# A hybrid decoder layer in f32: x, norm gains and conv weights come from the host in columns, and the norm of x and the k/v evacuation run as steps of the second product

## The chip, the cores and the metric

The kernel runs on one core of one Trainium2 chip. The metric is the time of one execution on the device, in microseconds (us); a kernel's figure is the median of its runs. Engines are named as in the profile: PE is TensorE (PEld its weight loads), DVE is VectorE, ACT is ScalarE, POOL is GpSimd, SP is SyncE. Loads and stores are put on a queue by an engine; in this kernel SP issues nearly all of them, POOL a few.

## The reference

One layer of a decoder, with all arrays in f32. x has 256 rows and 2048 columns. RMSNorm divides by the root of the mean square of a row and multiplies by a gain.

```python
h = rms_norm(x, norm_mix_pre)
c_q, c_kv, k_r, q_s, k_s, v_s, gates = split(h @ w_in)   # 512 | 256 | 64 | 2048 | 256 | 256 | 4096 columns
A = mla_attention(...)      # 16 heads from the latents c_q, c_kv; dense causal, rotary part
B = swa_attention(q_s, k_s, v_s, sinks, rel_bias)        # 32 heads on 4 k/v heads, window 128
y = (sigmoid(gA) * (A @ w_o_mla) + sigmoid(gB) * (B @ w_o_swa)) @ w_out
x = x + rms_norm(y, norm_mix_post)
a, b = split(rms_norm(x, norm_ffn_pre) @ w_up)           # 2 x 5632
c = conv_b + sum_j conv_w[j] * shift(a, 2 - j)           # causal, width 3
x = x + rms_norm((gelu(c) * b) @ w_down, norm_ffn_post)
```

## The kernel before

**Products.** Each f32 product is made of three products in the fp32r type: an operand is split into a rounded part (hi) and the rest (lo), and `mm3` (L142 to L145) adds hi times hi, lo times hi and hi times lo into one accumulator. In the profile's names the weights are `whi` and `wlo`, the activations `ah` and `al` (later bh, gh and so on), and L143, L144, L145 are the three products of a 128x128 activation tile with a 128x512 weight tile. The activations are the stationary operand, in columns: the features lie on the 128 partitions and the 256 rows of x are two tiles of 128 columns. So x has to be transposed before the first product.

**Weights.** `wchunk` (L101) issues the load of one piece of weights on SP's queue into a tile `raw<n>` (512 KB: two k-tiles of 128x512; n counts through the whole kernel), ACT copies it to `whi` (L118) and DVE subtracts to get `wlo` (L119). There are RAW = 3 raw tiles, so the load of raw n waits until the `wlo` of n-3 has been made, and RING = 5 tiles of whi and of wlo.

**The order.** `gemm` (L147) walks over the 16 k-tiles of one block of 512 weight columns: load, split, then 6 products per k-tile (two row tiles times three). After each load it calls `tick`, which runs what `at(n, ...)` put into the table `steps` for load n: the evacuations, small products and softmax pieces of other stages are placed between the loads in this way. On DVE, ACT and SP the written order holds inside the block `tc.manual_schedule`; elsewhere a scheduler orders the instructions by what they depend on, and `keep_in_program_order` holds single ones where they are written.

**The head,** which the change touches. Twelve small bf16 products (`warm_up`) run on PE while the first data come, then the gain of the first norm (`grow`, 16x128) is transposed into columns of `gmat` by `columns` (transpose on PE, L235, copy on DVE), then 15 more small products. The first product of the kernel, raw0 to raw8 (raw0 and raw1 hold one k-tile each, 256 KB), gives the k and v columns of the sliding-window attention (C_KS). x comes in rows as four tiles `xc` of 256x512 between the weight loads. For each k-tile, `x_cols` makes two transposes on PE (`xt`, L256), and `split_to` (L197) makes `ah` on ACT (times the gain, L203) and `al` on DVE. The norm's factor isn't needed for that: the row's 1/rms is multiplied into the results when they leave the accumulators. `x_square` (L246) takes the squares and their sums on ACT, one xc at a time, tile `junk`. Behind the product `x_norm` makes the factor r1 on DVE, transposes the other gains (`grow2`) and the conv weights (`cvr`, into `cvT`), and makes the relative-bias strip `strip` (product `pstrip`, L285, copy, store to DRAM, on POOL's queue; later read back shifted as `bias`, L377). Then k and v leave the accumulators as `kd` and `vs` (ACT L307 and L310, and a half of kd on DVE).

The second product, raw9 to raw16, is the first 512 of the 2048 q columns of the sliding-window attention. Steps in it: `swa_v(t)` (product `vr` with `flip`, which reverses the rows, L316, split into `vx`) at its loads 0 and 1, and `swa_k(g)` (products `kt`, L323, split into `kx`) at its loads 2 to 5. The third product starts with raw17.

The tiles of ah and al (`xth`, `xtl`) and those of later activations (`oth`, `otl`) are reserved one behind the other in `base`, with small unused tiles `line_a` (24 columns of 4 bytes) and `line_b` (8) between them, which set at which address the tiles behind them start.

Of the kernel before, what the change touches and what calls it, by code (L numbers as in the profile page):

```python
# [19 lines left out]
P = 128  # L20
# [21 lines left out]
def trunk_layer(ctx, tc, x, g_mix_pre, g_mix_post, g_ffn_pre, g_ffn_post, w_in, g_q, w_q, g_kv, w_kv,  # L42
                sinks, rel, wo_a, wo_b, w_out, w_up, conv_w, conv_b, w_down, rope_tab, strip_sel, out):
# [18 lines left out]

    ident = sb(base, [P, P], "ident")
# [23 lines left out]
    gmat = sb(base, [P, 40], "gmat")  # L87
# [121 lines left out]
    grow = sb(p0, [16, P], "grow")  # L209
    nc.sync.dma_start(grow, g_mix_pre.rearrange("(k p) -> k p", p=P))  # L210
    xc = []

    def load_x(c):
        t = sb(p0, [P, NT, 512], f"xc{c}")
        nc.sync.dma_start(t, x[:, c * 512:(c + 1) * 512].rearrange("(t p) n -> p t n", p=P))
        xc.append(t)

    load_x(0)
    grow2 = sb(p0, [24, P], "grow2")
    pool.dma_start(grow2[0:16, :], g_ffn_pre.rearrange("(k p) -> k p", p=P))  # L220
    pool.dma_start(grow2[16:20, :], g_q.rearrange("(k p) -> k p", p=P))
    pool.dma_start(grow2[20:22, :], g_kv.rearrange("(k p) -> k p", p=P))
    cvr = [sb(p0, [88, P], f"cvr{i}") for i in range(2)]
    cw3 = conv_w.rearrange("j (k p) -> j k p", p=P)
    pool.dma_start(cvr[0][0:44, :], cw3[0])
    pool.dma_start(cvr[0][44:88, :], cw3[1])
    pool.dma_start(cvr[1][0:44, :], cw3[2])
    pool.dma_start(cvr[1][44:88, :], conv_b.rearrange("(k p) -> k p", p=P))
    pool.dma_start(rtab, rope_tab.rearrange("(t p) a b -> p t a b", p=P))
    pool.dma_start(sink, sinks.partition_broadcast(P))  # L230
    cvT = sb(base, [P, 176], "cvT")

    def columns(dst, rows, n):
        pg = pss.tile([P, 512], F32, name=f"pg{rows.tensor.name}", tag="s")
        ins = pe.transpose(pg[:, 0:n], rows[0:n, :], ident[0:n, 0:n])  # L235
        tc.keep_in_program_order(ins)
        vec.tensor_copy(dst, pg[:, 0:n])

    sb(base, [P, 24], "line_a")
# [3 lines left out]

    def x_square(c):
        for t in range(NT):
            act.activation(junk, xc[c][:, t, :], AF.Square, accum_out=ssx[:, t, c:c + 1])  # L246

    def x_cols(k, ke):
        if k in (1, 6, 10):
            load_x(len(xc))  # L250
        if k and k % 4 == 0:
            x_square(k // 4 - 1)
        for k in range(k, ke):
            pt = (pst, pss)[k % 2].tile([P, 512], F32, name=f"xt{k}", tag="ts"[k % 2])
            for t in range(NT):
                ins = pe.transpose(pt[:, t * P:(t + 1) * P], xc[k // 4][:, t, (k % 4) * P:(k % 4 + 1) * P], ident)  # L256
                if k == 0:
                    tc.keep_in_program_order(ins)
            split_to(XH(k), XL(k), pt[:, 0:256], gmat[:, k:k + 1])
# [5 lines left out]
    junk = sb(p0, [P, 512], "junk", tag="junk", bufs=2)  # L265
# [7 lines left out]
    pool.dma_start(sel, strip_sel)  # L273

    def x_norm():
# [3 lines left out]
        columns(gmat[:, 16:38], grow2, 22)  # L279
        for i in range(2):  # L280
            columns(cvT[:, i * 88:(i + 1) * 88], cvr[i], 88)
        vec.tensor_scalar(r1s, r, 0.125, None, op0=ALU.mult)
        vec.tensor_scalar(rh, r, 0.5, None, op0=ALU.mult)
        pp = pss.tile([P, 512], F32, name="pstrip", tag="s")
        tc.keep_in_program_order(pe.matmul(pp[0:SH, 0:384], relx, sel, start=True, stop=True))  # L285
# [4 lines left out]
    with tc.manual_schedule(engines={mybir.EngineType.DVE, mybir.EngineType.Activation, mybir.EngineType.SP}):  # L290
        columns(gmat[:, 0:16], grow, 16)
        warm_up(WARM[1])
        acc, _ = gemm(XH, XL, w_in, 0, KT, C_KS, 512, pre=x_cols)
        x_square(3)
    r1 = x_norm()
    es0.close()


# [704 lines left out]
```

## Time and profile before

| | |
|---|---|
| median of 3 runs | 1501.5 us (1501.39 to 1504.84) |
| the profiled execution | 1502.09 us, span 1500.3 us |
| granted TensorE clock, mean | 0.998 |
| busy share of the span | PE 99%, PEld 83%, DVE 63%, ACT 53%, POOL 4% |
| moved by DMA | 285.46 MB, mean 190 GB/s |
| on the chain that ended last | PE 92%, DVE 3%, ACT 2%, DMA 2%, issue 1% |
| raw loads of 512 KB from w_in | 111 of this form, 4.2 us from issue to landing |

The span is what lies between the first and the last recorded instruction; the execution's time has 1.8 us around it. Busy times of matmuls overlap (a product is listed with 377 to 394 ns, though they follow each other faster), so a busy PE is not by itself a PE at its peak. The chain is followed back from the last instruction to what released each step. In tables of windows an engine's cell is its busy time with the count of instructions. In the timeline a line gives the start, the duration, the engine, the line of the kernel, the operation and tile, and in brackets what was waited for and how long.

### The profile page before, as it was taken

What the parts mean: (1) busy time and instruction counts of PE and PEld (TensorE: products, weight loads), DVE (VectorE), ACT (ScalarE), POOL (GpSimd) and SP (SyncE); (2) the same over time, 40 slices, a digit from 0 to 9 for tenths busy, and PEclk for the clock granted to TensorE, in tenths of its full rate; (3) what the DMA queues carried; (4) which work ended last, traced back from release to release, by engine and by line L of the source; (5) the groups of instructions that cost most, each with busy time, mean ns of one, the idle gap of its engine ahead of it and who ended that gap; (6) DMA issues with size and microseconds to landing.
All of it is one profiled execution on the core that took longest, in us unless ns stands there. A gap on an engine that the chain in (4) does not pass through costs nothing.

```text
span 1500.3 us, 20157 instructions
## 1 busy us (share of the span) xinstructions
PE 1483.9 (99%) x7347; PEld 1245.4 (83%) x7347; DVE 940.6 (63%) x1607; ACT 800.6 (53%) x1289; POOL 62.0 (4%) x105
## 2 busy tenths in 40 slices
PE   8999999999999999999999999999999999999997
PEld 6888887888899988888888888888888888888887
DVE  5688884444767764655666666666544466666755
ACT  6588874434555553444555555555444455545542
POOL 2123210000000001000000000000000000000000
PEclk9999999999999999999999999999999999999999
DMA  7776656776655559766656666665666666665563
GB/s 235 221 178 166 166 161 202 207 207 209 183 156 163 161 167 314 241 210 203 197 177 184 187 190 185 185 183 183 196 192 190 194 184 182 189 189 183 182 196 113
DMA packets 161748, 285.46 MB, mean 190 GB/s; under 512 B 18468, under 2 KB 33942, under 8 KB 161521
## 3 DMA queue, kind: packets, MB, share of 16 engines
q1 hardware_dynamic: 156464, 267.96, 59.2%
q0 software_dynamic: 5184, 16.22, 4.5%
q8 instruction: 58, 0.95, 0.3%
q14 instruction: 42, 0.34, 0.1%
HBM read 277.79 MB, written 6.34 MB: 189 GB/s over the span
## 4 chain that ended last, share of the span: by engine, by line
PE 92%; DVE 3%; ACT 2%; DMA 2%; issue 1%; SPq 0%; DVEq 0%; ACTq 0%
PE accg L145 27%; PE accg L144 27%; PE accg L143 27%; DMA raw<-in_w_in_dram 2%; PE fT L847 1%; DVE wlo L119 1%; PE mpo L681 1%; PE ms L647 1%; ACT p L407 1%; ACT whi L118 1%; PE qn L610 1%; PE qn L612 1%; PE qn L611 1%; PE ms L652 0%; PE ptm L365 0%
## 5 line engine op out<-in xcount | busy, mean ns | idle before, releaser
L119 DVE TENSOR_TENSOR wlo<-raw,whi 128x1024 fp32r<-128x1024 f32 (+2 forms) x501 | 609.1, 1217 | 482.9 <-ACT whi L118 482.1
L118 ACT CAST whi<-raw 128x1024 fp32r<-128x1024 f32 (+2 forms) x501 | 523.0, 1045 | 588.5 <-PE accg L145 500.2
L143 PE MATMUL accg<-whi,bh 128*128 128x512 f32 x960 | 377.9, 394 | 0.0
L145 PE MATMUL accg<-whi,bl 128*128 128x512 f32 x960 | 374.6, 390 | 0.0
L144 PE MATMUL accg<-wlo,bh 128*128 128x512 f32 x960 | 374.0, 390 | 0.0
L143 PE MATMUL accg<-whi,ah 128*128 128x512 f32 (+2 forms) x896 | 344.2, 385 | 0.7 <-ACT whi L118 0.7
L144 PE MATMUL accg<-wlo,ah 128*128 128x512 f32 (+2 forms) x896 | 341.4, 381 | 0.5 <-DVE wlo L119 0.5
L145 PE MATMUL accg<-whi,al 128*128 128x512 f32 (+2 forms) x896 | 340.9, 380 | 0.0
L145 PEld LDWEIGHTS accg<-whi,bl 128*128 128x128 f32 x960 | 180.2, 188 | 38.1
L144 PEld LDWEIGHTS accg<-wlo,bh 128*128 128x128 f32 x960 | 180.4, 188 | 36.4
L143 PEld LDWEIGHTS accg<-whi,bh 128*128 128x128 f32 x960 | 180.3, 188 | 36.0
L145 PEld LDWEIGHTS accg<-whi,al 128*128 128x128 f32 x896 | 168.5, 188 | 31.5
L144 PEld LDWEIGHTS accg<-wlo,ah 128*128 128x128 f32 x896 | 168.6, 188 | 30.8 <-DVE wlo L119 1.7
L143 PEld LDWEIGHTS accg<-whi,ah 128*128 128x128 f32 x896 | 168.5, 188 | 30.4 <-ACT whi L118 1.6
L143 PE MATMUL accg<-whi,gh 128*128 128x512 f32 (+1 forms) x104 | 39.3, 378 | 0.0
L144 PE MATMUL accg<-wlo,gh 128*128 128x512 f32 (+1 forms) x104 | 38.8, 373 | 0.0
L145 PE MATMUL accg<-whi,gl 128*128 128x512 f32 (+1 forms) x104 | 38.3, 373 | 0.0
L407 ACT ACTIVATE p<-p,nm 128x128 f32<-128x128 f32 x64 | 28.4, 445 | 5.9 <-DVE nm L398 5.9
L847 PEld LDWEIGHTS fT<-ident,f 128*128 128x128 f32 x176 | 21.8, 140 | 5.7
L847 PE MATMUL fT<-ident,f 128*128 128x128 f32 x176 | 26.3, 272 | 0.0
L851 ACT ACTIVATE cc<-fT,cvT 128x256 f32<-128x256 f32 x44 | 24.2, 550 | 0.0
L143 PEld LDWEIGHTS accg<-whi,gh 128*128 128x128 f32 x104 | 19.6, 188 | 4.1 <-ACT gh L200 0.9
(302 smaller groups left out, 1279.6 us busy)
## 6 DMA issues: line engine op xcount, KB each, us to landing
raw<-in_ffn_w_up_dram SPq DMA_DIRECT2D x176, 512.0 KB, 4.3
raw<-in_w_in_dram SPq DMA_DIRECT2D x111, 512.0 KB, 4.2
raw<-in_ffn_w_down_dram SPq DMA_DIRECT2D x88, 512.0 KB, 3.8
raw<-in_w_o_swa_dram SPq DMA_DIRECT2D x32, 512.0 KB, 4.2
raw<-in_w_o_mla_dram SPq DMA_DIRECT2D x32, 512.0 KB, 4.8
raw<-in_w_out_dram SPq DMA_DIRECT2D x32, 512.0 KB, 4.1
raw<-in_mla_w_q_up_dram SPq DMA_DIRECT2D x48, 128.0 KB, 2.9
bias<-strip POOLq DMA_DIRECT2D x16, 256.0 KB, 4.0
```

What stands on the lines that cost most here:

```text
L118: act.copy(hi[:, :n], raw[:, :n])
L119: vec.tensor_tensor(lo[:, :n], raw[:, :n], hi[:, :n].bitcast(F32), op=ALU.subtract)
L143: pe.matmul(o, ah, bh, start=start, stop=False)
L144: pe.matmul(o, ah, bl, start=False, stop=False)
L145: pe.matmul(o, al, bh, start=False, stop=stop)
L407: act.activation(pb[:, i, a:b], pb[:, i, a:b], AF.Exp, bias=st["nm"][:, i, t:t + 1], accum_out=st["sm"][:, i, t:t + 1])
L610: pe.matmul(o, wh, ch(k), start=k == 0, stop=False)
L611: pe.matmul(o, wh, cl(k), start=False, stop=False)
L612: pe.matmul(o, wl, ch(k), start=False, stop=k == nk - 1)
L647: pe.matmul(o, w, v_, start=n == 0, stop=False)
L847: pe.transpose(pt[:, q * 256 + t * P:q * 256 + (t + 1) * P], sa[t][q][:, i * P:(i + 1) * P], ident)
L851: act.activation(cc, a, AF.Identity, scale=w2, bias=cb_)
```

## The change

The host now hands over x a second time in columns (`x_cols`, 128 x 4096, all 2.10 MB), the four gains as one array of 128 x 38 (`gain_cols`) and the conv weights and bias as 128 x 176 (`conv_cols`). The tile `xr` takes x in columns, in pieces that fit the weight loads; gmat and the first two pieces are issued on ACT's queue, the others on SP's. ACT and DVE split from xr, where they split from the transposes' results before. x in rows (`xc`) is still loaded, for the squares alone, and later: beside raw5, raw6, raw7 and behind raw8. A copy of one column (`first`) stands first on ACT. All transposes of the head go, with the loads grow, grow2 and cvr and the copies behind them.

The squares of xc0 stand at the last piece of the first product; those of xc1, xc2 and xc3, the norm, and the evacuation of k and v become steps of the second product at its loads 0, 1, 2 and 3, `swa_v` moves to its loads 4 and 5, `swa_k` to 4 to 7. The written order now holds on DVE, ACT and SP from the kernel's start to the end of the first product. rtab (the rotary table) is loaded at step 4, cvT at step 20. The pads change: line_b from 8 to 32 columns, and a new line_w of 8 behind the tiles `oth` and `otl`. The tiles for activations start 32 bytes later than before, those for weights 160 bytes later.

```diff
@@ trunk_layer(...)
+    head = ExitStack()
+    head.enter_context(tc.manual_schedule(engines={mybir.EngineType.DVE, mybir.EngineType.Activation, mybir.EngineType.SP}))
...
-    grow = sb(p0, [16, P], "grow")
-    nc.sync.dma_start(grow, g_mix_pre.rearrange("(k p) -> k p", p=P))
+    xcut = [0, 1, 2] + list(range(4, KT + 1, 2))
+    xr = sb(p0, [P, KT, 256], "xr")
+    def load_xt(i, q):
+        if i < len(xcut) - 1:
+            k, ke = xcut[i], xcut[i + 1]
+            q.dma_start(xr[:, k:ke, :], x_cols_in[:, k * 256:ke * 256].rearrange("p (k n) -> p k n", n=256))
+    first = sb(base, [P, 1], "first")
+    nc.scalar.dma_start(gmat, gain_cols)
+    load_xt(0, nc.scalar)
+    load_xt(1, nc.scalar)
+    act.copy(first, ident[:, 0:1])
...
-    load_x(0)
-    grow2 = sb(p0, [24, P], "grow2")
-    pool.dma_start(grow2[0:16, :], g_ffn_pre.rearrange("(k p) -> k p", p=P))
...
-    pool.dma_start(cvr[1][44:88, :], conv_b.rearrange("(k p) -> k p", p=P))
-    pool.dma_start(rtab, rope_tab.rearrange("(t p) a b -> p t a b", p=P))
-    pool.dma_start(sink, sinks.partition_broadcast(P))
     cvT = sb(base, [P, 176], "cvT")
-    def columns(dst, rows, n):
-        pg = pss.tile([P, 512], F32, name=f"pg{rows.tensor.name}", tag="s")
-        ins = pe.transpose(pg[:, 0:n], rows[0:n, :], ident[0:n, 0:n])
-        tc.keep_in_program_order(ins)
-        vec.tensor_copy(dst, pg[:, 0:n])
-    sb(base, [P, 24], "line_a")
+    sb(base, [P, LINE_A], "line_a")                  # LINE_A = 24
...
     def x_cols(k, ke):
-        if k in (1, 6, 10):
-            load_x(len(xc))
-        if k and k % 4 == 0:
-            x_square(k // 4 - 1)
-        for k in range(k, ke):
-            pt = (pst, pss)[k % 2].tile([P, 512], F32, name=f"xt{k}", tag="ts"[k % 2])
-            for t in range(NT):
-                ins = pe.transpose(pt[:, t * P:(t + 1) * P], xc[k // 4][:, t, (k % 4) * P:(k % 4 + 1) * P], ident)
-            split_to(XH(k), XL(k), pt[:, 0:256], gmat[:, k:k + 1])
+        i = xcut.index(k)
+        if i:
+            load_xt(i + 1, nc.sync)
+        if i in (5, 6, 7):
+            load_x()
+        if i == 8:
+            x_square(0)
+        for k in range(k, ke):
+            split_to(XH(k), XL(k), xr[:, k, :], gmat[:, k:k + 1])
...
+    pool.dma_start(sink, sinks.partition_broadcast(P))
+    def x_strip():
+        pp = pss.tile([P, 512], F32, name="pstrip", tag="s")
+        pe.matmul(pp[0:SH, 0:384], relx, sel, start=True, stop=True)
+        vec.tensor_copy(sel[0:SH, :], pp[0:SH, 0:384])
+        pool.dma_start(strip, sel[0:SH, :])
     def x_norm():
...
-        columns(gmat[:, 16:38], grow2, 22)
-        for i in range(2):
-            columns(cvT[:, i * 88:(i + 1) * 88], cvr[i], 88)
         vec.tensor_scalar(r1s, r, 0.125, None, op0=ALU.mult)
         vec.tensor_scalar(rh, r, 0.5, None, op0=ALU.mult)
-        pp = pss.tile([P, 512], F32, name="pstrip", tag="s")
-        tc.keep_in_program_order(pe.matmul(pp[0:SH, 0:384], relx, sel, start=True, stop=True))
-        vec.tensor_copy(sel[0:SH, :], pp[0:SH, 0:384])
-        pool.dma_start(strip, sel[0:SH, :])
...
-    with tc.manual_schedule(engines={mybir.EngineType.DVE, mybir.EngineType.Activation, mybir.EngineType.SP}):
-        columns(gmat[:, 0:16], grow, 16)
-        warm_up(WARM[1])
-        acc, _ = gemm(XH, XL, w_in, 0, KT, C_KS, 512, pre=x_cols)
-        x_square(3)
-    r1 = x_norm()
+    warm_up(WARM[1])
+    acc_kv, _ = gemm(XH, XL, w_in, 0, KT, C_KS, 512, pre=x_cols)
+    load_x()
+    head.close()
+    def swa_begin():
+        nonlocal es1, p1, r1
+        x_square(3)
+        r1 = x_norm()
+        es0.close()
...
-    for t in range(NT):
+    def swa_kv(t):
         kk = sb(p1, [P, 4, 2, 64], f"kd{t}", tag="qx", bufs=2)
-        a3 = acc[t].rearrange("p (a b) -> p a b", b=64)
+        a3 = acc_kv[t].rearrange("p (a b) -> p a b", b=64)
...
     steps.clear()
+    at(0, lambda: x_square(1), x_strip)
+    at(4, lambda: tc.keep_in_program_order(pool.dma_start(rtab, rope_tab.rearrange("(t p) a b -> p t a b", p=P))))
+    at(20, lambda: tc.keep_in_program_order(pool.dma_start(cvT, conv_cols_in)))
+    at(1, lambda: x_square(2))
+    at(2, swa_begin)
     for t in range(NT):
-        at(t, lambda t=t: swa_v(t))
+        at(3, lambda t=t: swa_kv(t))
+        at(4 + t, lambda t=t: swa_v(t))
     for g in range(4):
-        at(2 + g, lambda g=g: swa_k(g))
-    sb(base, [P, 8], "line_b")
+        at(4 + g, lambda g=g: swa_k(g))
+    sb(base, [P, LINE_B], "line_b")                  # LINE_B = 32
...
+    sb(base, [P, LINE_W], "line_w")                  # LINE_W = 8, behind oth and otl
@@ kernel(...)
+    add("x_cols", np.asarray(inputs["x"])[0].T.reshape(KT, P, S).transpose(1, 0, 2).reshape(P, KT * S), False)
+    add("gain_cols", np.concatenate([_columns(inputs[n][0]) for n in
+                                     ("norm_mix_pre", "norm_ffn_pre", "mla_q_norm", "mla_kv_norm")], 1), False)
+    add("conv_cols", np.concatenate([_columns(inputs["ffn_conv_w"][0]), _columns(inputs["ffn_conv_b"][0])], 1), False)
```

What the change makes of the order is shown at three places. First SP's queue, from its first load on, which carries weights (raw) and x. Before:

```order
L210 DMA grow_115<-in_norm_mix_pre_dram 16x128
L215 DMA xc0_117<-in_x_dram 128x2x512
L116 DMA raw0_187<-in_w_in_dram 128x512
L215 DMA xc1_193<-in_x_dram 128x2x512
L116 DMA raw1_206<-in_w_in_dram 128x512
L116 DMA raw2_228<-in_w_in_dram 128x2x512
L116 DMA raw3_258<-in_w_in_dram 128x2x512
L215 DMA xc2_264<-in_x_dram 128x2x512
L116 DMA raw4_288<-in_w_in_dram 128x2x512
```

And after, from its fifth load on (the four ahead of it are raw0, a piece of xr, raw1 and another piece):

```order
L118 DMA raw2_203<-in_w_in_dram 128x2x512
L217 DMA xr_117<-in_x_cols_dram 128x512
L118 DMA raw3_226<-in_w_in_dram 128x2x512
L217 DMA xr_117<-in_x_cols_dram 128x512
L118 DMA raw4_249<-in_w_in_dram 128x2x512
L217 DMA xr_117<-in_x_cols_dram 128x512
L229 DMA xc0_256<-in_x_dram 128x2x512
L118 DMA raw5_274<-in_w_in_dram 128x2x512
L217 DMA xr_117<-in_x_cols_dram 128x512
L229 DMA xc1_281<-in_x_dram 128x2x512
L118 DMA raw6_299<-in_w_in_dram 128x2x512
L217 DMA xr_117<-in_x_cols_dram 128x512
```

The rows of x that stood ahead of raw0 and between the first loads now stand at raw5 and behind, and a piece of xr stands between every two raw loads.

Second, ACT at the end of the first product: ah is the split of x, junk the squares, whi the rounded weights. Before:

```order
L118 CAST whi6_350<-raw6_348 128x1024
L246 ACTIVATE junk_153,ssx_149<-xc2_264 128x512 x2
L203 ACTIVATE ah6_139<-xt12_356,gmat_106 128x256
L203 ACTIVATE ah6_139<-xt13_361,gmat_106 128x256
L118 CAST whi7_380<-raw7_378 128x1024
L203 ACTIVATE ah7_140<-xt14_384,gmat_106 128x256
L203 ACTIVATE ah7_140<-xt15_389,gmat_106 128x256
L118 CAST whi8_408<-raw8_406 128x1024
L246 ACTIVATE junk_153,ssx_149<-xc3_324 128x512
L118 CAST whi9_498<-raw9_496 128x1024
L246 ACTIVATE junk_153,ssx_149<-xc3_324 128x512
```

And after:

```order
L120 CAST whi7_326<-raw7_324 128x1024
L246 ACTIVATE junk0_0_330,ssx_141<-xc0_256 128x512
L246 ACTIVATE junk0_1_332,ssx_141<-xc0_256 128x512
L205 ACTIVATE ah7_132<-xr_117,gmat_108 128x256 x2
L120 CAST whi8_352<-raw8_350 128x1024
L246 ACTIVATE junk1_0_409,ssx_141<-xc1_281 128x512
L246 ACTIVATE junk1_1_411,ssx_141<-xc1_281 128x512
L120 CAST whi9_393<-raw9_391 128x1024
L246 ACTIVATE junk2_0_435,ssx_141<-xc2_306 128x512
L120 CAST whi10_419<-raw10_417 128x1024
L246 ACTIVATE junk2_1_437,ssx_141<-xc2_306 128x512
L246 ACTIVATE junk3_0_457,ssx_141<-xc3_368 128x512
```

The squares of xc0 now stand between whi7 and the split and cast for raw8, and the squares of the other three lie behind whi8, from the start of the second product on.

Third, PE in the second product, where the reversal of v (vr) stands between the products of a load. Before:

```order
L143 MATMUL accg_9_1_495<-whi10_520,ah1_134 128x512
L144 MATMUL accg_9_1_495<-wlo10_521,ah1_134 128x512
L316 MATMUL vr0_514<-vs0_470,flip_99 128x256
L145 MATMUL accg_9_1_495<-whi10_520,al1_142 128x512
L316 MATMUL vr1_536<-vs1_475,flip_99 128x256
L143 MATMUL accg_9_0_494<-whi11_542,ah2_135 128x512
L144 MATMUL accg_9_0_494<-wlo11_543,ah2_135 128x512
L145 MATMUL accg_9_0_494<-whi11_542,al2_143 128x512
L143 MATMUL accg_9_1_495<-whi11_542,ah2_135 128x512
```

And after:

```order
L146 MATMUL accg_9_1_390<-wlo13_519,ah4_129 128x512
L147 MATMUL accg_9_1_390<-whi13_518,al4_137 128x512
L312 MATMUL vr0_535<-vs0_509,flip_101 128x256
L319 MATMUL kt0_539<-flip_101,kd1_511 128x128
L319 MATMUL kt0_539<-flip_101,kd0_506 128x128
L319 MATMUL kt0_539<-flip_101,kd1_511 128x128
L145 MATMUL accg_9_0_389<-whi14_547,ah5_130 128x512
L146 MATMUL accg_9_0_389<-wlo14_548,ah5_130 128x512
L147 MATMUL accg_9_0_389<-whi14_547,al5_138 128x512
```

vr0 stood between the products with whi10 and whi11; it now stands ahead of those with whi14, with the first kt group behind it. vr1 (before between the products with whi10 too) now stands ahead of those with whi15. On ACT, kd and vs stand two raw loads later than before: kd0 stood behind whi12 and now stands behind whi14, vs0 behind whi13 and now behind whi15.

## What is to be expected

> **What bounds the kernel now.** First the page: its busy shares, its slices and its chain.
>
> ```profile
> PE 1483.9 (99%) x7347; PEld 1245.4 (83%) x7347; DVE 940.6 (63%) x1607; ACT 800.6 (53%) x1289; POOL 62.0 (4%) x105
> ...
> PE   8999999999999999999999999999999999999997
> ...
> PE 92%; DVE 3%; ACT 2%; DMA 2%; issue 1%; SPq 0%; DVEq 0%; ACTq 0%
> ```
>
> TensorE carries the time and only the first slice (37.5 us) is below 9, which is where this change works. So the head is cut by stages. Columns: length, busy time of PE, PEld, DVE, ACT and POOL with counts, granted clock, busy share of the DMA engines, GB/s.
>
> ```profile
> 0.00:4.00 4.00, 1.95 (x17) 1.72 (x18) 0.72 (x3) 0.00 (x0) 3.42 (x15) 1.00 0.36 79
> 4.00:8.00 4.00, 2.94 (x24) 2.31 (x21) 1.02 (x2) 2.64 (x4) 3.19 (x7) 1.00 0.95 324
> 8.00:12.00 4.00, 3.46 (x15) 2.17 (x14) 2.03 (x5) 1.92 (x4) 1.04 (x2) 1.00 1.04 337
> 12.00:16.00 4.00, 3.38 (x17) 2.40 (x15) 2.54 (x4) 3.87 (x9) 0.00 (x0) 1.00 0.99 329
> 16.00:20.00 4.00, 4.00 (x22) 3.19 (x21) 2.85 (x4) 3.10 (x7) 0.00 (x0) 1.00 0.97 347
> 20.00:24.00 4.00, 4.00 (x21) 3.30 (x20) 2.73 (x5) 2.57 (x6) 0.00 (x0) 1.00 0.58 146
> 24.00:28.00 4.00, 4.00 (x21) 3.27 (x20) 2.48 (x5) 3.75 (x8) 0.00 (x0) 1.00 0.60 162
> ...
> 1100.00:1150.00 50.00, 50.00 (x222) 41.41 (x221) 23.68 (x20) 19.58 (x19) 0.00 (x0) 1.00 0.64 197
> ```
>
> The head has two regimes: until 20 us the DMA engines are full (0.95 to 1.04) and PE has gaps; from 20 us PE is full and DMA is at 0.6. The last row prices a 128x512 product: 50 us / 222 = 0.226 us. Then the rows where a stage begins or ends, from the timeline (start, duration).
>
> ```profile
> 7.48 0.50 PE L143 MATMUL accg<-whi,ah 128*128 128x512 f32 x1 [0.41 <-ACT whi L118]
> ...
> 35.07 0.23 PE L235 MATMUL pggrow<-ident,grow 22*128 22x22 f32 x1
> ...
> 36.54 0.83 PE L285 MATMUL pstrip<-sel,relx 33*32 33x384 f32 x2
> 37.30 0.50 PE L144 MATMUL accg<-wlo,ah 128*128 128x512 f32 x1
> ...
> 41.51 0.39 PE L144 MATMUL accg<-wlo,ah 128*128 128x512 f32 x1
> 42.00 0.70 PE L316 MATMUL vr<-vs,flip 128*128 128x256 f32 x2
> 42.35 0.58 PE L145 MATMUL accg<-whi,al 128*128 128x512 f32 x1
> 42.77 0.59 PE L316 MATMUL vr<-vs,flip 128*128 128x256 f32 x2
> 43.01 0.58 PE L143 MATMUL accg<-whi,ah 128*128 128x512 f32 x1
> ```
>
> The first product runs from 7.48 to 35.07; the product with raw11 starts at 43.01, with vr0 and vr1 already paid. From there PE is gapless to the end of the second product:
>
> ```profile
> 43.01:62.20 19.19, 19.19 (x98) 16.27 (x97) 11.07 (x13) 9.74 (x14) 2.86 (x4) 1.00 0.81 245
> ```
>
> After it every engine's order is the same in both kernels but for one small load (cvT) on POOL. So the forecast is: at what time does the second product end, 62.2 before.
>
> **The change part by part.** Prices of the pieces:
>
> ```profile
> 22.60 0.44 PE xt L256 x4
> L203 ACT ACTIVATE ah<-xt,gmat x16: 454/470/478, 6.4 to 29.6; 128x256 fp32r<-128x256 f32 x16
> L200 ACT CAST ah<-uu x32: 397/403/405, 808.5 to 1365.8; 128x256 fp32r<-128x256 f32 x32
> L246 ACT ACTIVATE junk<-xc x8: 629/632/641, 12.4 to 32.5; 128x512 f32<-128x512 f32 x8
> L246 ACT ACTIVATION_READ_ACCUMULATOR junk<-xc x8: 186/188/196, 12.9 to 33.0; 128x1 f32 x8
> L119 DVE TENSOR_TENSOR wlo<-raw,whi x14: 693/1226/1226, 7.5 to 41.7; 128x1024 fp32r<-128x1024 f32 x12, 128x512 fp32r<-128x512 f32 x2
> L118 ACT CAST whi<-raw x14: 619/1047/1053, 9.2 to 43.1; 128x1024 fp32r<-128x1024 f32 x13, 128x512 fp32r<-128x512 f32 x1
> DMA to landing us min/median/max: 3.6/4.4/6.1
> ```
>
> *PE.* 32 transposes at 0.11 us go, 3.5 us; so do the three gain and conv transposes at 35.07 to 36.3 and the stall behind them, about 1 us. What stays is 192 products x 0.226 = 43.4 us, pstrip 0.75, vr0 and vr1 0.8 and four kt groups 2.7: 47.7 us.
>
> *DMA.* x now comes in columns (2.10 MB) for the products and again in rows (2.10 MB) for the squares. Up to raw7 the stream is 2.10 MB of columns, three xc (1.57) and raw0 to raw7 (3.67): 7.34 MB. strip and rtab (0.31) follow pstrip into the first product on POOL's queue; seven small loads leave POOL. Before, 0.08 x 4 + 0.324 x 4 = 1.6 MB had moved at 8 us, and the next three stages moved 329 to 347 GB/s, with POOL's small pieces in them and a stretch where SP stood behind a raw slot. I take 370, between these and the stream's better moments:
>
> ```profile
> GB/s 378 412 381 403 393 354 323 263 253 239 270 348 375 348 369 375 378 371 401 360 310 330 348 253 178 253 335 369 416 396 396 416 389 362 232 191 307 375 403 253
> ```
>
> (40 slices of 8 to 20 us; most are 348 to 416, dips to 178.) Raw7's last byte is then at 8 + (7.34 + 0.3 - 1.6)/0.37 = 24.3, and with 0.7 us to its semaphore raw7 lands at 25.0. The ends are 27 (338 GB/s and 1 us) and 24 (400). By the Trainium skill's DMA: Bandwidth & Descriptors, section "Where 436 GB/s comes from", loads from HBM are bound near 358 GB/s when both cores of a pair stream, and one core alone was measured at 425. No run here separates the two; by 425 raw7 would land near 23, and the sum would be that of the second rival.
>
> *SP.* The columns and xc are queued between the raw loads, behind their slot waits:
>
> ```profile
> SPq L116 <- DVE wlo L119: 26.2, 12, 2.9
> ```
>
> A blocked SP does not starve the stream while 3 to 4 MB lie issued ahead, as they do until raw8; so nothing for that wait. The first three loads go to ACT's queue, which issues nothing before: 3 issues at 0.4 to 0.5 us like SP's, before ACT has any work. gmat (128 pieces of 152 B) lies between these two:
>
> ```profile
> grow<-in_norm_mix_pre_dram SPq DMA_DIRECT2D x1, 8.0 KB, 1.6
> sink<-in_swa_sinks_dram POOLq DMA_DIRECT2D x1, 16.0 KB, 4.7
> ```
>
> So the first product's matmul comes at 6 to 7 us instead of 7.48. That gain is lost again: raw2 lands near 9.7 and its split ends at 12, before which PE has only 12 matmuls.
>
> *ACT.* Per raw load it does two ah (0.40 to 0.47 each, now from SBUF; 0.85 kept) and whi 1.05, under PE's 12 x 0.226 = 2.7. But the squares, spread over the first product before, now bunch behind raw7: xc0 between whi7 and whi8, xc1 to xc3 in the second product, 1.45 us each. Nothing covers the first, so from raw7 on ACT and DVE lead: whi7 26.05, wlo7 27.3, PE done 29.6; square 27.5, ah 28.35, whi8 29.4, wlo8 30.65, and ten matmuls behind it: the first product ends at 32.9 (35.07 before). Square xc1 30.85, whi9 31.9, wlo9 33.15, PE 35.65; raw10 hides its square, PE 38.4. So raw11's product starts at 38.4.
>
> *The moved evacuation.* kd and vs move two raw loads later on ACT and vr0 three on PE. ACT has time there, but vs0 stands behind whi15 on ACT and vr0 stands ahead of raw14's products on PE. PE reaches vr0 at 38.4 + 3 x 2.72 = 46.6. raw15 is issued when wlo12 frees its slot, about 38.8: lands 43.2 at the median of 4.4, vs0 at 44.7. But the bias loads, held until the last square, now go out at about 36 beside it, and beside them raw loads took longer before:
>
> ```profile
> 43.78 0.74 POOL L377 DMA_DIRECT2D bias<-strip  x1 [4.02 <-PE vr L316]
> ...
> DMA to landing us min/median/max: 5.4/6.6/7.3
> ```
>
> At 7.3 vs0 comes at 47.6. So PE waits 0 to 1.0 us; I take 0.5.
>
> *Sum.* 38.4 + 19.2 (rows as before) + 0.8 (vr0, vr1) + 0.5 = 58.9 against 62.2: 3.3 us less. The profiled execution took 1502.09 (span 1500.3), 0.6 over the median of 1501.5, so the median after is 1498.2. The bounds of the stream's rate alone make it 1.5 to 4.3 us.
>
> **The rivals.**
>
> *The transposes were hidden anyway.* They lay in front of a DMA-full stretch until 20 us, and the stream grows by 2.1 MB. At 338 GB/s raw7 lands 1.8 later, and vr0's wait is 1.0: the gain is 1 us, 1500.5. For it are the three stages at 329 to 347; against it, that the stream stood still in some of their slices.
>
> *PE bounds the head.* With the stream at 400 to 425 PE is gapless from raw2's split on: 12.0 + 11 x 0.226 + six loads x 2.72 + pstrip, then raw9 and raw10, gives raw11 at 37.0 and a gain of about 5: 1496.5. If the first loads also land earlier it goes on toward the floor, 6.4 + 47.7 = 54.1, a gain of 8: 1493.4. For it are the slices over 400; against it, ACT's chain of 5.6 us from raw7 to wlo8.
>
> *Slower: the shifted tiles.* The pads and the new tile move every tile behind them by 32 or 160 bytes. If a start address matters to what PE reads, it is paid in all 5880 products of a 512-wide kind:
>
> ```profile
> L143 PE MATMUL accg<-whi,bh 128*128 128x512 f32 x960 | 377.9, 394 | 0.0
> ...
> L145 PEld LDWEIGHTS accg<-whi,bl 128*128 128x128 f32 x960 | 180.2, 188 | 38.1
> L144 PEld LDWEIGHTS accg<-wlo,ah 128*128 128x128 f32 x896 | 168.6, 188 | 30.8 <-DVE wlo L119 1.7
> ```
>
> (3 x (960 + 896 + 104) = 5880.) One ns each is 5.9 us; from 1.3 ns more (0.6%) the kernel is slower by 0.3%, at 1506. Against it: weight loads from tiles far apart take 188 ns alike.
>
> *Slower: the clock.* It is 1.00 in every stage above, with PE busy 3.38 of 4 us. If longer waits dropped it to half, 16 us at half pace would lose the gain and 4.5 us more: 1506. The Trainium skill, TensorE: Matmul & The Clock Gate, Part 1, has the clock halve after an idle window of about 3.4 us; by that rule waits of 1 to 2 us leave it alone, and the trace agrees as far as it goes.
>
> **How the numbers follow.** A measurement of this kernel tells 0.3%, 4.5 us, from no change. The ACT- and DMA-led head (gain 2 to 4.5) gets 0.43, transposes hidden anyway (0 to 2) 0.13: 0.56 within 0.3%. PE bounds the head gets 0.29, and 0.03 goes to addresses that suit better: 0.32 faster. Shifted tiles get 0.08, the clock 0.04: 0.12 slower. The range reaches from nearly PE's floor, 1494, past no gain to 1503; it leaves out the slower cases and the floor's tail, together under 0.18.
>
> **What would show it.** After: no xt rows; DMA share near 1 up to 25 us, not 20; raw7 landing at 24 to 27; a wait of PE for wlo behind the first square; raw11's product at 37 to 41.5 and the second product's end at 57 to 61; vr0 waiting for vs0 by at most 1 us; 0.226 us per product unchanged at 1100 us. I am wrong if the second product ends before 57 or after 62, or if the time past it changes by over 1 us.

## The result: 25 us slower, and the profile after

The changed kernel takes 1526.28 us (median of 4, 1523.62 to 1527.61) against 1501.45 us: 1.0158 times the time before, 95% interval 1.0137 to 1.0178 (the ratio goes by all executions, not by the two medians). The forecast was 1498.2 us, with 1494 to 1503 as its range. The profiled execution took 1525.49 us, span 1523.7 us. In all the runs below one execution alone falls out: one of the eleven of a_biaslate took 4365.73 us, which its ratio leaves out and its median keeps.

The page of the changed kernel, the lines that answer to those of before:

```profile
PE 1507.3 (99%) x7311; PEld 1246.1 (82%) x7311; DVE 940.2 (62%) x1603; ACT 799.8 (52%) x1290; POOL 59.1 (4%) x99
...
PE   9999999999999999999999999999999999999997
...
PEclk9999999999999999999999999999999999999999
DMA  9776566666655558766555566655556665655563
...
PE 94%; DVE 2%; ACT 2%; DMA 1%; issue 1%; DVEq 0%; ACTq 0%; SPq 0%
```

PE runs 36 matmuls fewer and is busy 23.4 us longer (1507.3 against 1483.9). The granted clock is at 9 in every slice. The first slice, 8 before, is 9: PE is busier in the head. So the loss is where nothing was changed. The rows of the wlo tiles (one line of before, one of after; the first and the last start are the two last times) say the same:

```profile
L119 DVE TENSOR_TENSOR wlo<-raw,whi x501: 693/1225/1609, 7.5 to 1477.8; 128x1024 fp32r<-128x1024 f32 x164, 128x640 fp32r<-128x640 f32 x2, 128x512 fp32r<-128x512 f32 x1
```

```profile
L121 DVE TENSOR_TENSOR wlo<-raw,whi x501: 692/1225/1622, 6.2 to 1500.9; 128x1024 fp32r<-128x1024 f32 x164, 128x640 fp32r<-128x640 f32 x2, 128x512 fp32r<-128x512 f32 x1
```

The changed kernel is 1.3 us ahead at its first weights and 23.1 us behind at its last. In the same two views, the first product of wlo with bh still starts 0.6 us ahead (254.2 against 254.8), the first with gh 14.6 us behind (1058.6 against 1044.0): the loss grows through the kernel. The timeline of PE shows how, at one block of the down product, far behind the change. 96 products whose stationary tile is ah lie between the first row and the second (before):

```profile
1120.18 0.39 PE L143 MATMUL accg<-whi,ah 128*128 128x512 f32 x1
...
1141.94 0.39 PE L143 MATMUL accg<-whi,gh 128*128 128x512 f32 x1
```

The same block in the changed kernel, and behind it 48 products with gh, up to the third row:

```profile
1135.92 0.40 PE L145 MATMUL accg<-whi,ah 128*128 128x512 f32 x1
...
1158.24 0.40 PE L145 MATMUL accg<-whi,gh 128*128 128x512 f32 x1
...
1169.16 0.40 PE L145 MATMUL accg<-whi,bh 128*128 128x512 f32 x1
```

Before: 21.76 / 96 = 0.2267 us per product. After: 22.32 / 96 = 0.2325 us with ah, but 10.92 / 48 = 0.2275 us with gh, in the same loop, from the same rings of weights, right behind it. Whether a product is slow depends on which tile is stationary.

### The profile page after: what moved, and what is told of

Its sections match the earlier page's. It is cut to its first block, busy times and chain, and to the rows that moved or that the text cites. A ratio compares the mean times of both kernels' runs of the same rounds, so it can differ in the third digit from the quotient of the medians.

```text
span 1523.7 us, 20082 instructions
## 1 busy us (share of the span) xinstructions
PE 1507.3 (99%) x7311; PEld 1246.1 (82%) x7311; DVE 940.2 (62%) x1603; ACT 799.8 (52%) x1290; POOL 59.1 (4%) x99
## 4 chain that ended last, share of the span: by engine, by line
PE 94%; DVE 2%; ACT 2%; DMA 1%; issue 1%; DVEq 0%; ACTq 0%; SPq 0%
PE accg L145 28%; PE accg L146 28%; PE accg L147 28%; PE fT L850 1%; DMA raw<-in_w_in_dram 1%; PE mpo L684 1%; PE ms L650 1%; DVE wlo L121 1%; PE qn L613 0%; PE qn L615 0%; PE qn L614 0%; ACT p L410 0%; PE pt L368 0%; PE ms L655 0%; ACT whi L120 0%
## 5 line engine op out<-in xcount | busy, mean ns | idle before, releaser
L145 PE MATMUL accg<-whi,bh 128*128 128x512 f32 x960 | 382.6, 399 | 0.0
L147 PE MATMUL accg<-whi,bl 128*128 128x512 f32 x960 | 379.1, 395 | 0.0
L146 PE MATMUL accg<-wlo,bh 128*128 128x512 f32 x960 | 379.0, 395 | 0.0
L145 PE MATMUL accg<-whi,ah 128*128 128x512 f32 (+2 forms) x896 | 347.8, 389 | 1.1 <-ACT whi L120 1.1
L146 PE MATMUL accg<-wlo,ah 128*128 128x512 f32 (+2 forms) x896 | 345.8, 386 | 0.0
L147 PE MATMUL accg<-whi,al 128*128 128x512 f32 (+2 forms) x896 | 344.9, 385 | 0.0
L147 PE MATMUL accg<-whi,gl 128*128 128x512 f32 (+1 forms) x104 | 38.4, 374 | 0.0
```

The lines of the kernel that those rows point to most:

```text
L145: pe.matmul(o, ah, bh, start=start, stop=False)
L146: pe.matmul(o, ah, bl, start=False, stop=False)
L147: pe.matmul(o, al, bh, start=False, stop=stop)
```

## The experiments

In what follows a slot is the time from the start of one 512-wide product to the start of the next, taken from the trace, those over 300 ns left out. "Distance" is the address of whi less that of ah (al lies at the same distance), bh or gh in a partition, modulo 256 bytes; whi and wlo are a multiple of 256 apart in all kernels but one. Every other tile of a ring or group is a multiple of 512 bytes further, so one number holds for all of them. A trace holds no addresses: the distances are worked out from the sizes and the order of the tiles in each kernel. The ratio is to the kernel before, measured beside it.

| kernel | distance ah, bh, gh | mean slot ah, bh, gh, ns | median us | ratio, 95% interval |
|---|---|---|---|---|
| before | 0, 0, 0 | 227.8, 227.4, 227.3 | 1501.5 | |
| after | 128, 128, 0 | 232.7, 233.0, 227.8 | 1526.28 | 1.0158 (1.0137 to 1.0178) |
| a_line16 | 128, 128, 0 | 232.7, 232.9, 227.5 | 1527.71 | 1.0169 (1.0153 to 1.0184) |
| b_line32 | 0, 0, 0 | 227.9, 227.5, 227.3 | 1501.77 | 1.0002 (0.9993 to 1.0011) |
| a_act96_w0 | 160, 160, 0 | 234.2, 234.3, 227.6 | 1530.61 | 1.0190 (1.0175 to 1.0205) |
| a_act0_w96 | 224, 224, 0 | 233.2, 233.3, 227.3 | 1527.96 | 1.0177 (1.0160 to 1.0194) |
| a_rel0 | 0, 0, 0 | 227.8, 227.5, 227.3 | 1501.57 | 0.9999 (0.9990 to 1.0008) |
| b_w128 | 128, 128, 0 | 232.7, 233.0, 227.7 | 1526.21 | 1.0161 (1.0147 to 1.0174) |
| a_ah0_bh128 | 0, 128, 0 | 227.8, 233.0, 227.3 | 1517.43 | 1.0102 (1.0089 to 1.0116) |
| b_32_64 | 64, 32, 0 | 229.6, 233.2, 227.4 | 1520.26 | 1.0120 (1.0106 to 1.0134) |
| b_96_192 | 192, 96, 0 | 233.3, 233.4, 227.9 | 1527.90 | 1.0175 (1.0161 to 1.0189) |

Names with a start from the changed kernel, those with b from the kernel before.

**Where a tile starts.** The first four runs changed pads alone. The theory was that the start addresses, which the change moved from 96 to 0 modulo 128, cost the time.

```diff
-LINE_A = 24
+LINE_A = 16
```

> The changed kernel with line_a cut from 24 to 16 columns: activation tiles and weight tiles again start at 96 modulo 128 bytes, as before the change; nothing else differs from the changed kernel. Theory (start addresses cost 4 to 5 ns per 512-wide product): the pitch of products at 1100 us falls from 0.229 to 0.225 us per instruction, the time to about 1500, 1 to 2 us under the kernel before. Rival (the pitch comes from the changed instruction stream or the new use of ACT's queue): it stays at 1524 to 1528.

```diff
-    sb(base, [P, 24], "line_a")
+    sb(base, [P, 32], "line_a")
```

> The kernel before with line_a raised from 24 to 32 columns: every tile from the activations on starts 32 bytes later, at 0 modulo 128, nothing else changes. Address theory: about 1526, 25 us slower, with a pitch of 0.229 us at 1100 us. Rival (instruction stream): 1501, as before.

The next is a_line16 with 8 columns more behind the tiles oth and otl:

```diff
-LINE_A = 24
+LINE_A = 16
-LINE_W = 8
+LINE_W = 16
```

> The changed kernel with the activation tiles (the stationary operand) at 96 modulo 128 and the weight tiles (the moving operand) left at 0. If the stationary operand's address matters: about 1500. If the moving operand's does: about 1526. If the difference of the two matters (0 in both kernels): something else again, up or down.

```diff
-LINE_W = 8
+LINE_W = 32
```

> The changed kernel with the activation tiles left at 0 modulo 128 and the weight tiles at 96. The mirror of the run above: stationary operand matters, about 1526; moving operand matters, about 1500.

The theory fell. With all tiles back at 96 modulo 128 nothing came back (a_line16), and with all at 0 the kernel before lost nothing (b_line32). Neither operand's own place was it: in the last two the activations or the weights stood where the kernel before has them, and both were slow, by different amounts. What the table's first six rows leave is the third case of the expectation, the difference of the two addresses, but with 256 as the modulus: 0 in the two fast kernels, 128, 160 and 224 in the four slow ones, and 0 for gh in all six, whose slot is 227.3 to 227.8 ns in all six.

**The distance.** The next four put this to the test, against the rival that the changed instruction stream is the cause, in both directions.

```diff
-LINE_W = 8
+LINE_W = 40
```

> The changed kernel with line_w raised from 8 to 40 columns: the weight tiles move by 128 bytes, so that the address of whi less that of ah, bh or gh is a multiple of 256, as in the kernel before (in the changed kernel it is 128 modulo 256 for ah and bh, 0 for gh). Theory A (the distance modulo 256 between the stationary and the moving operand sets the pitch): 0.226 us per product everywhere, the head alone differs, about 1499, 2 to 3 us faster than before. Theory B (the instruction stream or ACT's queue): 1525 to 1531 as with every pad so far. Theory C (the absolute start of the weight tiles): 1525 to 1531 too, since 0 modulo 256 has only been good in one kernel.

In the kernel before, b_w128 adds behind the tiles oth and otl:

```diff
+    sb(base, [P, 32], "line_w")
```

> The kernel before with a pad of 32 columns behind the tiles oth and otl: weight tiles move by 128 bytes against ah and bh, gh moves with them, nothing else. Theory A: about 1526, the pitch near 232 ns with ah and bh and 227 with gh, as in the changed kernel. Theories B and C: 1501.5.

The next keeps LINE_W at 8:

```diff
-LINE_B = 32
+LINE_B = 64
```

> The changed kernel with line_b raised from 32 to 64 columns: the distance is 0 modulo 256 for ah and 128 for bh. Theory A: products with ah at 227 ns, those with bh at 232 to 233; half of the loss comes back, about 1512. Theory B: 1526 with no difference between ah and bh.

```diff
-    sb(base, [P, 8], "line_b")
+    sb(base, [P, 16], "line_b")
+    sb(base, [P, 8], "line_w")
```

> The kernel before with 8 columns more in line_b and 8 columns behind oth and otl: the distance is 64 modulo 256 for ah and 32 for bh. Theory A: slower than before, with pitches of their own for ah and bh between 227 and 235 ns; how they depend on the distance is open. Theories B and C: 1501.5 with both at 227.

In all four the slots came as the distance theory has them. Two times did not: a_rel0 was expected 2 to 3 us faster than before and is as fast, and a_ah0_bh128, expected near 1512, takes 1517.43 us. One pad of 128 bytes takes the whole loss away (a_rel0); the same pad in the kernel before, with none of the change, makes the whole loss (b_w128, 1526.21 us against the 1526.28 of the changed kernel). The kernel with mixed distances shows it inside one trace; these are the first rows of a block of bh, of the block of ah behind it, and of the next one of bh (timeline of a_ah0_bh128):

```profile
253.73 0.40 PE L145 MATMUL accg<-whi,bh 128*128 128x512 f32 x1
...
276.05 0.40 PE L145 MATMUL accg<-whi,ah 128*128 128x512 f32 x1
...
297.84 0.40 PE L145 MATMUL accg<-whi,bh 128*128 128x512 f32 x1
```

96 products each: 22.32 us with bh at 128 and 21.79 us with ah at 0, with the same rings of raw, whi and wlo. The last of the map:

```diff
-    sb(base, [P, 8], "line_b")
+    sb(base, [P, 32], "line_b")
+    sb(base, [P, 24], "line_w")
```

> The kernel before with 24 columns more in line_b and 24 columns behind oth and otl: the distance between moving and stationary operand is 192 modulo 256 for ah and 96 for bh (0 for gh). Theory (the distance modulo 256 alone): ah, whose distance is 64 below a multiple, near the 229 to 230 ns that 64 gave, or near the 233 of 224; bh near the 232 to 234 of 128 and 160; the whole between 1515 and 1530. If the distance didn't matter: 1501.5.

Both distances are slow, at 233.3 and 233.4 ns. Of the eight distances in steps of 32, 0 is fast, 64 costs 2 ns, and the six others cost 5 to 7 ns; the guess that 192 might be as mild as 64 was wrong.

**Which two reads.** In a_al128 and a_ah128 only one of the two stationary tiles is off. Each has a pad behind the tiles of ah; a_al128 has 32 more in line_b, and both start from a_rel0, as the third does.

```diff
+    sb(base, [P, 32], "line_m")
     xtl = [slot_a(p, "l") for p in range(8)]
```

> The changed kernel with all distances at 0 modulo 256 but for al, at 128 (a pad of 32 columns between the tiles of ah and al, and 32 more in line_b). The three products of ah are whi with ah, wlo with ah, whi with al. If the loss arises while the next stationary tile is loaded beside the running product: the step from wlo,ah to whi,al is slow (about 234 to 240 ns) and the two others stay at 227. If it arises inside a product between its own two operands: the step from whi,al to the next whi,ah is slow. bh at 227 in any case. Time: 900 products at 6 to 15 ns more, 1506 to 1515.

> All distances at 0 modulo 256 but for ah, at 128 (a pad of 32 columns between the tiles of ah and al, nothing else). With al alone at 128 two of the three steps were slow: wlo,ah to whi,al (al is loaded beside the running wlo) and whi,al to whi,ah (al is the running product's own). Load only: whi,ah to wlo,ah and whi,al to whi,ah slow, wlo,ah to whi,al at 227. Own only: whi,ah to wlo,ah and wlo,ah to whi,al slow. Either: all three slow, at about 232 to 234, and the time above the 1508.8 of the run with al, at 1510 to 1513.

The third takes wlo out of step with whi:

```diff
         hi = (own or ring).tile([P, 1024], F32R, name=f"whi{i}", tag="whi")
+        if i == 0:
+            ring.tile([P, 32], F32, name="line_r", tag="line_r", bufs=1)
         lo = (own or ring).tile([P, 1024], F32R, name=f"wlo{i}", tag="wlo")
```

> Distances of whi to ah, al, bh and bl at 0 modulo 256, those of wlo at 128 (a pad of 32 columns between the rings of whi and wlo); for gh and gl, which lie behind the rings, the other way round: whi 128, wlo 0. All readings with the distance of the operands: in ah and bh the step wlo to whi,al or whi,bl slow (about 232 to 237), the two others at 227; in gh the steps of whi slow and that of wlo fast. Time: a third of the loss, 1508 to 1512. If only whi's place mattered: ah and bh at 227 throughout.

Mean slots of the three products of a k-tile, in ns, beside those of a_rel0:

| kernel | whi,ah | wlo,ah | whi,al | whi,bh | wlo,bh | whi,bl | median us | ratio, 95% interval |
|---|---|---|---|---|---|---|---|---|
| a_rel0 | 227.7 | 227.8 | 227.7 | 227.7 | 227.4 | 227.4 | 1501.57 | 0.9999 (0.9990 to 1.0008) |
| a_al128 | 228.1 | 232.3 | 233.7 | 227.7 | 227.4 | 227.4 | 1508.77 | 1.0047 (1.0033 to 1.0061) |
| a_ah128 | 233.3 | 232.6 | 234.1 | 227.3 | 227.2 | 227.4 | 1511.54 | 1.0066 (1.0053 to 1.0080) |
| a_wlo128 | 233.8 | 232.8 | 230.5 | 235.3 | 233.8 | 230.2 | 1525.03 | 1.0153 (1.0137 to 1.0169) |

With al alone off, two slots are slow: the one in which al is loaded, and the one of the product that uses it. With ah alone off, all three are. Both agree with "a slot is slow when the tile being loaded or the product's own is off the moving one". The third run breaks that rule: only the product of wlo should have been slow, and all three were, at nearly the whole loss. For gh, which in that kernel stands at a multiple of 256 from wlo and 128 from whi, the slots are 232.5 (whi,gh), 226.2 (wlo,gh) and 228.2 (whi,gl). So what is shown is this: the kernel is fast when all four of ah, al, whi and wlo are multiples of 256 apart, and in the three runs with ah, al or wlo alone out of step products in which that tile takes no part are slow too. Which reads meet stays open.

The Trainium skill, TensorE: Matmul & The Clock Gate, "Step-by-step: what each phase is for", has loading the next stationary tile take no read bandwidth from the running product, through a port of its own. The weight loads themselves agree (188 ns in both kernels, below). The slots speak against it: with al alone moved, the slot of wlo,ah, in which al is only loaded, grows from 227.8 to 232.3 ns. As a_wlo128 fits no rule yet, that isn't proof.

**The head.** a_rel0 has the whole change at the old distances, so it is the change without its accident. The trace is ahead of before by 1.2 us at the first weights and 2.5 at the last (1475.3 against 1477.8), but these are single executions; the medians differ by 0.2 us and the interval is 0.9990 to 1.0008. So by the median the change without its accident gains nothing that these runs can tell from zero. In the timeline of PE a wait stood in the second product (a_rel0):

```profile
48.49 0.67 PE L312 MATMUL vr<-vs,flip 128*128 128x256 f32 x2 [2.29 <-issue]
```

Three runs, each from a_rel0, tried to take it away. In a_vlate the steps are one load later:

```diff
-        at(4 + t, lambda t=t: swa_v(t))
+        at(5 + t, lambda t=t: swa_v(t))
-        at(4 + g, lambda g=g: swa_k(g))
+        at(5 + g, lambda g=g: swa_k(g))
```

> The changed kernel with all distances at 0 and swa_v and swa_k one raw load later (steps 5 and 6, 5 to 8). In the second product PE waits 2.3 us before vr0. Theory 1 (vr0 waits for vs0, which stands behind the cast of raw15 on ACT): the wait shrinks to below 1 us and about 1.5 us are gained, 1498.5 to 1500.5. Theory 2 (raw14 and raw15 land late, beside the bias loads, and PE has no weights): the wait only changes its name, no gain, 1500 to 1502.

The wait before vr0 is gone, but 1.12 us before a kt came in its place (timeline of a_vlate), and the median is 1502.48, ratio 1.0005 (0.9996 to 1.0014): no gain.

```profile
58.45 0.94 PE L319 MATMUL kt<-flip,kd 128*128 128x128 f32 x6 [1.12 <-DVE kx L203]
```

In a_biaslate and a_biasall the first two bias loads are held back by a small copy; this is the copy of the first, that of the second covers columns 255 and 256 and so both parts of a bias tile.

```diff
             st["bias"] = sb(p1, [P, 2, 384], f"bias{u}", tag="bias", bufs=2)
+            if u < 2:
+                vec.tensor_copy(st["bias"][:, :, 0:1], vx[0][:, 0:2, 0, 0:1].bitcast(F32))
```

> The changed kernel with all distances at 0 and the first two bias loads held until vx0 is there (one 2-element copy each on DVE into the bias tile): they start at about 52 us, where they start at 35.5. Both theories: raw14 to raw16 land 3.6 to 4.7 us after their issue, where they took 7.3 to 8.7; PE's wait before vr0 falls from 2.3 to below 0.5 us; about 2 us gained, 1498 to 1500, unless the bias loads then hold up raw18 to raw20 in the same way.

> Both parts of the first two bias loads held until vx0 (before, one part of each still went at 35.5 us and the wait before vr0 was gone, with 1.3 us of wait for kx at 55 us in its place). Raw14 to raw16 land 3.6 to 4.7 us after their issue; in the trace 0.3 to 1 us earlier than the run with one part held, at load 30 about 3.3 us ahead of the kernel before. Median 1499 to 1501; if what the trace shows of the head is real in the median, below 1500.

Time from issue to landing of the raw loads issued between 34 and 48 us, first in the changed kernel, then in a_biasall:

```profile
DMA to landing us min/median/max: 4.4/7.8/8.8
```

```profile
DMA to landing us min/median/max: 4.0/4.4/5.2
```

The bias loads were what held the weights up, and with them away vr0 follows the products without a wait (timeline of a_biasall):

```profile
45.95 0.60 PE L312 MATMUL vr<-vs,flip 128*128 128x256 f32 x2
```

With one part held, PE waits 1.31 us for kx before a kt group at 55.16 us in its place; with both, that wait is gone too, and the third product starts at 57.62 us, where it starts at 60.52 in a_rel0. The medians are 1500.89 (one part held, 0.9995, 0.9985 to 1.0004; 1498 to 1500 was expected) and 1500.15 us (both, 0.9993, 0.9984 to 1.0001). The second is the fastest version of the study, but its interval still holds "no change", and it isn't below 1500 as the expectation had it if the trace's 3 us were real.

## Why the prediction was wrong

The step that failed is the one from "After it every engine's order is the same in both kernels" to "at what time does the second product end": the forecast put everything past the second product at no change. It takes 24.7 us more there, from the third product's first row (62.34 before, shown here; 60.66 after, shown below) to the last product of the kernel.

```profile
62.34 0.39 PE L143 MATMUL accg<-whi,ah 128*128 128x512 f32 x1
```

Summed over the two traces, the 512-wide products with bh make 15.5 us of that, those with ah 8.5, all else 0.7. The cause was named, and priced too low in chance: "Slower: the shifted tiles", 0.08. It had the size within reach (1 ns is 5.9 us; the products got 5 to 6 ns longer; of the 5880 that it counts, 5544 are 512 wide and 264 of these are with gh), but looked at the wrong quantity and at the wrong evidence.

- The quantity. It asked whether "a start address matters to what PE reads" and spoke of a shift of 32 and 160 bytes. What counts is the difference of the two shifts, 128 bytes, against a modulus of 256, which only the runs showed. Both shifts stood in the text; one subtraction would have shown that every product of ah and bh changes its distance.
- The evidence against it, "weight loads from tiles far apart take 188 ns alike", says nothing on slots. In the slow kernel the load's row is the same while the product's is longer:

```profile
L145 PE MATMUL accg<-whi,bh 128*128 128x512 f32 x960 | 382.6, 399 | 0.0
...
L145 PEld LDWEIGHTS accg<-whi,bh 128*128 128x128 f32 x960 | 180.5, 188 | 40.8
```

- "0.226 us per product unchanged at 1100 us" failed: 218 products in the 50 us where 222 stood before. That the time past the second product might change was named as what would make the forecast wrong.

```profile
1100.00:1150.00 50.00, 50.00 (x218) 40.75 (x217) 23.43 (x20) 20.09 (x20) 0.00 (x0) 1.00 0.60 191
```

Of the head the prediction had the times up to raw11, but not the path to them, and one term of the rest too small. These are the rows of the changed kernel: the first weights, the split of raw8 and its first products, the starts of the product with raw9 and with raw11, the wait, the start of the last kt group and that of the third product.

```profile
6.21 0.79 PE L145 MATMUL accg<-whi,ah 128*128 128x512 f32 x1 [1.10 <-ACT whi L120]
...
26.89 1.03 ACT L120 CAST whi<-raw 128x1024 fp32r<-128x1024 f32 x1
27.96 1.23 DVE L121 TENSOR_TENSOR wlo<-raw,whi 128x1024 fp32r<-128x1024 f32 x1 [0.45 <-ACT whi L120]
29.92 0.63 PE L145 MATMUL accg<-whi,ah 128*128 128x512 f32 x2
30.39 0.40 PE L146 MATMUL accg<-wlo,ah 128*128 128x512 f32 x1
...
32.72 0.40 PE L145 MATMUL accg<-whi,ah 128*128 128x512 f32 x1
...
38.32 0.40 PE L145 MATMUL accg<-whi,ah 128*128 128x512 f32 x1
...
48.77 0.67 PE L312 MATMUL vr<-vs,flip 128*128 128x256 f32 x2 [1.89 <-issue]
...
60.07 0.83 PE L319 MATMUL kt<-flip,kd 128*128 128x128 f32 x6
60.66 0.48 PE L145 MATMUL accg<-whi,ah 128*128 128x512 f32 x1
```

- The start: 6 to 7 us forecast, 6.21 measured. The end of the first product: 32.9 forecast, 32.72. The product with raw11: 38.4 forecast, 38.32.
- The last two agree by luck. The forecast had ACT and DVE lead behind raw7, with wlo8 done at 30.65. In the trace raw7 landed at 23.8 and not 25.0 (the 0.7 us to a semaphore in that sum is shown by no run), whi8 and wlo8 were done at 27.92 and 29.19, and PE came to raw8 only at 29.92. It waited for nothing between 6.21 and 46.89; the wait for wlo behind the first square didn't come. This is the rival "PE bounds the head". Its 37.0 for raw11 was missed by 1.3 us, 0.7 of it in the 107 products up to there at 232.7 ns, where 226 were taken.
- The DMA engines are full until 28 us, as said ("near 1 up to 25 us"); at 367 GB/s, where 370 was taken:

```profile
6.00:23.00 17.00, 16.79 (x57) 12.39 (x58) 11.86 (x20) 11.28 (x20) 0.16 (x1) 1.00 1.02 367
...
24.00:28.00 4.00, 4.00 (x19) 3.22 (x18) 2.63 (x6) 4.00 (x9) 0.10 (x1) 1.00 1.04 377
28.00:32.00 4.00, 4.00 (x18) 3.21 (x18) 2.41 (x2) 3.51 (x8) 0.00 (x0) 1.00 0.75 239
```

- "PE waits 0 to 1.0 us; I take 0.5" failed: 1.89 us. The reason given was right (the bias loads beside raw15, vs0 behind its cast), but the end of the range was too low: 7.3 us was the longest of the raw loads beside the same four bias loads before. The bias loads now start at 35.35 us, just ahead of raw14 (35.72), and raw14 to raw16 took up to 8.8 us (the row of raw loads shown above).

```profile
35.35 0.72 POOL L380 DMA_DIRECT2D bias<-strip  x1 [11.26 <-DMA raw<-in_w_in_dram]
```

- So the second product with its kt groups ends at 60.66, not 58.9: 1.4 from the wait, and 0.4 from 72 products at 5.8 ns more. Against 62.34 before (the prediction's 62.2 stops 0.14 short of it) 1.7 us are gained and not 3.3; at the old distances the gain in the median is 0.2 us, with an interval of about 1.4 us to either side.
- The clock, the other slower rival, has no part in the 24.7 us, but its column misled. It reads 1.00 in every stage, while the trace's record of the clock begins only at 12.71 us (5.08 before) and stays at 1.00 from there to 1517.98, behind the last product. Up to 12.65 us the products of the changed kernel follow each other at nearly half pace, 427 ns:

```profile
7.53 0.63 PE L147 MATMUL accg<-whi,al 128*128 128x512 f32 x1
7.95 0.63 PE L145 MATMUL accg<-whi,ah 128*128 128x512 f32 x1
...
12.22 0.62 PE L146 MATMUL accg<-wlo,ah 128*128 128x512 f32 x1
12.65 0.43 PE L147 MATMUL accg<-whi,al 128*128 128x512 f32 x1
```

  It cost the head little: in a_biaslate, where such slots end at 10.1 us, the product that starts here at 12.22 waited for raw2's wlo until 12.31. The prediction's "waits of 1 to 2 us leave it alone" holds behind the 1.89 us of the changed kernel, but in a_line16 the clock went to 0.50 behind a wait of 1.96 us at the same place, again with slots of 427 ns (a window of that run):

```profile
50.90:52.30 1.40, 1.40 (x5) 1.05 (x4) 0.52 (x2) 1.16 (x2) 0.00 (x0) 0.50 0.80 230
```

## What to carry to other kernels

A change that adds or drops a small tile moves every tile behind it: before any other reasoning, take the addresses of the moving and the stationary tiles in the old and the new build and compare their differences modulo 256 bytes, for the hi and lo parts alike; where they differ, the slot of every 512-wide product may change, and a pad restores it. The 192 products of 256 columns with ah, at the end of the kernel, don't show the cost (119.3 ns in the changed kernel, 120.0 before). When a change of the first 4% of a kernel comes out over 1% slower, look at the same unchanged block far behind it in both traces first: a slot of 232 against 227 ns is seen there in two rows, the first of the block and the first behind it. A granted clock of 1.00 at the very start of a trace is to be checked against the slots. A gain of 2 us in the trace of one execution says little where executions of one kernel spread over 2.5 to 5 us, as those of before, a_rel0 and a_biasall do.

## What the runs showed of the chip

A 512-wide product in fp32r follows the last one after 227 to 228 ns on average when the moving tiles and the stationary tiles are multiples of 256 bytes apart in a partition, and after 229.6 (64 bytes off) to 234 ns (160 off) otherwise, with the weight load's own row at 187 to 191 ns throughout and a granted clock of 0.996 to 0.999 over each run. Single slots differ by product rather than stretch evenly: the timeline of a_wlo128 repeats 0.24, 0.24 and 0.22 to 0.23 us, and with wlo and bh 96 bytes apart (b_96_192) the slots of wlo are at 237.0 ns on average, those of whi beside them at 231.6 and 231.3.

```profile
280.63 0.40 PE L148 MATMUL accg<-whi,ah 128*128 128x512 f32 x1
280.87 0.40 PE L149 MATMUL accg<-wlo,ah 128*128 128x512 f32 x1
281.11 0.39 PE L150 MATMUL accg<-whi,al 128*128 128x512 f32 x1
281.33 0.40 PE L148 MATMUL accg<-whi,ah 128*128 128x512 f32 x1
```

The Trainium skill, SBUF — State Buffer, "SBUF: two separate sides", says that PE never waits for another engine at its SBUF ports. The runs don't test that: what they show is a cost that goes with where PE's own operands lie to each other.
